# Expert stage of a hybrid block: the gather of token rows without transposes, two units at a time, in a written order

## The chip, the cores and the metric

The kernel runs on one core of one Trainium2 chip. The metric is the device time of one execution in microseconds (us). Engines are named as the profile names them: PE (TensorE matmul), PEld (its weight loads), DVE (VectorE), ACT (ScalarE), POOL (GpSimd), SP (the queue that issues the weight transfers).

## The reference

One block of a model with 256 tokens of 2048 features (float32): an adaptive norm, a wide projection, three mixers (stick-breaking attention, a diagonal state space layer, a chunked mLSTM), gated projections and an output projection, and then a mixture of 32 experts (4 groups of 8, two experts chosen per token inside the best group) and a last norm. The change is in the mixture:

```python
g_idx = jnp.argmax(g_logits, axis=-1)                       # best group of a token
top_v, top_i = lax.top_k(e_in_group, TOP_K)                 # two of its 8 experts
...
hid = jax.nn.silu(jnp.einsum('td,edf->tef', t, w1)) * jnp.einsum('td,edf->tef', t, w3)
y = jnp.einsum('tef,efd->td', hid * gates.astype(hid.dtype)[:, :, None], w2)
```

`t` is the normed and modulated row of a token; `w1`, `w3` are 32 x 2048 x 256, `w2` is 32 x 256 x 2048.

## The kernel before

Up to `x1`, the sum of the input and the gated mixers, the work is dense and is not touched. While `w_out` is multiplied, `split_x1` splits each 512 columns of `x1` into a high and a low part (`xs[0]`, `xs[1]`, type fp32r) so that later two fast products give the accuracy of float32: part 0 is an ACT copy, part 1 a DVE subtraction.

**Routing (the prologue).** After the last product of `w_out`, a written order for PE, DVE and ACT computes logits, the best group, the two experts and, per token and *list*, a rank. A list holds the tokens that choose one of two experts of a group (16 lists, up to 64 tokens each; more than 64 is handled in a branch that these inputs don't take). A *unit* `u` (8 of them) is two lists, so 128 rows. `mem` says whether a token is in a list, `rank` its place there.

**Gather.** `sel_unit(u)` builds a 0/1 matrix of 256 tokens x 128 places, four DVE operations of 64 columns. `Gather.rows(j)` multiplies it with `xs`: four products of 512 columns give 128 gathered rows of feature block `j` (512 features, four blocks). `scale(j)` (ACT) takes them out of PSUM and multiplies by the norm of each row, `norms()`; `turn(j)` transposes the four 128x128 pieces on PE (line 259, tile `xgT`); `finish(j)` applies the modulation of the features and writes four blocks of `XG`, two on ACT and two on DVE. The products of the experts need features on the partitions, hence the transposes. `gates()` fetches the weights of the rows, `back()` the transposed `sel` that brings results back to the tokens.

**Experts.** A unit is two *pairs* (`n` = 0 to 15, `u, el = divmod(n, 2)`); a pair is two experts, one for each list, and uses the two halves of the PE array, 64 columns each (`Pair.mm` issues each product twice, for h = 0 and h = 1 with `tile_position=(0, 64 * h)`). Per pair `mm_in(j)` for four blocks gives `h` (line 1397, float32, 512 columns), `hidden()` the activation, `hidden_turn()` two transposes and an ACT copy `hh`, and `mm_out(f, c)` for two halves of the hidden features and four column blocks gives `y` (line 1397 too). `combine_mm` brings the results of the unit before back to token order (`sc`), `combine_add` adds them to `x1`.

**Weights.** A pair reads 12 buffers of 1 MiB (`load_in`: 8, in two transfers each; `load_out`: 4). The ring (`moe_raw`) has 11 of them, all issued by SP in program order; a transfer starts when the product that last read its buffer has ended. So the first 11 are loaded ahead of the stage, and the rest follow the releases. The row `final_g` for the last norm is loaded by POOL into one of the ring's buffers (tag `raw`) when the last pair's `mm_in(3)` has released it.

**Order.** From the first pair on, the loop over `n` is written as in the diff, but a scheduler decides the order of each engine's instructions in it; the prologue and the last pair have a written order (`tc.manual_schedule`). PSUM has four buffers for `y` (`mm`) and four for all else (`ms`).

## Time and profile before

| | us |
|---|---|
| three runs | 1597.33, 1601.37, 1603.7 (median 1601.37) |
| the profiled execution | 1600.31 |
| its span, from the first to the last instruction | 1598.5 |
| the prologue (rank known to first expert product) | 1082.20 to 1093.02 |
| the pairs, first to last expert product | 1093.02 to 1579.79 |

The times of the profile count from the start of the span. Busy times of PE are of records that overlap, so the distance between starts says more than the length of one. Releasers of a wait are inferred from semaphores.

### The profile page before, as it was taken

What the parts mean: (1) busy time and instruction counts of PE and PEld (TensorE: products, weight loads), DVE (VectorE), ACT (ScalarE), POOL (GpSimd) and SP (SyncE); (2) the same over time, 40 slices, a digit from 0 to 9 for tenths busy, and PEclk for the clock granted to TensorE, in tenths of its full rate; (3) what the DMA queues carried; (4) which work ended last, traced back from release to release, by engine and by line L of the source; (5) the groups of instructions that cost most, each with busy time, mean ns of one, the idle gap of its engine ahead of it and who ended that gap; (6) DMA issues with size and microseconds to landing.
All of it is one profiled execution on the core that took longest, in us unless ns stands there. A gap on an engine that the chain in (4) does not pass through costs nothing.

```text
span 1598.5 us, 25021 instructions
## 1 busy us (share of the span) xinstructions
PE 1509.0 (94%) x10228; PEld 1140.2 (71%) x10228; DVE 1015.1 (64%) x1733; ACT 568.6 (36%) x755; POOL 39.0 (2%) x63
## 2 busy tenths in 40 slices
PE   4999999989999998999999999999999999999996
PEld 2999999888888988899999998874334433443332
DVE  0879997889879999999778866553213212222124
...
GB/s 343 386 348 305 319 191 222 220 223 261 247 300 265 229 264 231 273 264 264 263 308 327 318 267 241 207 228 257 414 413 412 413 402 374 412 392 411 404 412 183
DMA packets 172249, 488.13 MB, mean 305 GB/s; under 512 B 13876, under 2 KB 14048, under 8 KB 162784
## 3 DMA queue, kind: packets, MB, share of 16 engines
...
q0 software_dynamic: 3088, 12.14, 2.3%
...
q10 hardware_dynamic: 576, 1.05, 0.2%
...
## 4 chain that ended last, share of the span: by engine, by line
PE 54%; DVE 25%; DMA 10%; issue 6%; ACT 4%; POOL 0%; SPq 0%; ACTq 0%; DVEq 0%; POOLq 0%
PE h L1397 14%; PE y L1397 9%; DVE accr L353 5%; DMA adar<-in_w_ada_dram 4%; DVE g_sb_w L132 2%; DVE g_ml_w L132 2%; PE sc L1446 2%; PE wo_b L143 2%; PE wo_b L144 2%; PE wo_b L142 2%; DVE bu L698 2%; PE xg L1312 2%; DVE s5pp L695 2%; DVE bu L697 1%; DVE s5qq L696 1%
## 5 line engine op out<-in xcount | busy, mean ns | idle before, releaser
L1397 PE MATMUL h<-w,XG 128*64 128x512 f32 x1024 | 245.3, 599 | 0.0
L1397 PEld LDWEIGHTS h<-w,XG 128*64 128x64 f32 x1024 | 75.7, 137 | 139.1 <-issue 137.4
L353 DVE SCALAR_TENSOR_TENSOR accr<-adar,ccol,accr 128x1024 f32<-128x1024 f32 x120 | 153.5, 1280 | 18.2 <-DMA adar<-in_w_ada_dram 17.3
L1397 PE MATMUL y<-w,hh 128*64 128x512 f32 x512 | 150.4, 598 | 0.5 <-ACT hh L1419 0.5
L1410 DVE SCALAR_TENSOR_TENSOR s<-h,gg,s 128x256 f32<-128x256 f32 x16 | 7.7, 484 | 167.8 <-ACT s L1409 167.8
L1455 DVE TENSOR_TENSOR x<-x,sc 128x512 f32<-128x512 f32 x64 | 43.0, 682 | 105.7 <-PE sc L1446 105.7
L1397 PEld LDWEIGHTS y<-w,hh 128*64 128x64 f32 x512 | 49.0, 136 | 81.5 <-issue 77.7
L1409 ACT ACTIVATE s<-h 128x256 f32<-128x256 f32 x16 | 6.1, 383 | 212.3 <-PE h L1397 212.3
L144 PE MATMUL g_sb_b<-hT,g_sb_w 128*128 128x256 f32 x256 | 73.1, 285 | 8.5 <-DVE g_sb_w L132 8.4
L144 PE MATMUL g_ml_b<-hT,g_ml_w 128*128 128x256 f32 x256 | 72.4, 283 | 3.3 <-DVE g_ml_w L132 3.3
L1287 DVE TENSOR_SCALAR XG<-xgT,G,modc 128x128 f32<-128x128 f32 x64 | 26.0, 410 | 77.0 <-ACT XG L1284 77.0
L144 PE MATMUL g_s_b<-hT,g_s_w 128*128 128x256 f32 x256 | 72.1, 282 | 1.6 <-DVE g_s_w L132 1.4
L142 PE MATMUL g_ml_b<-hT,g_ml_w 128*128 128x256 f32 x256 | 72.4, 283 | 0.0
L142 PE MATMUL g_sb_b<-hT,g_sb_w 128*128 128x256 f32 x256 | 71.9, 281 | 0.0
L142 PE MATMUL g_s_b<-hT,g_s_w 128*128 128x256 f32 x256 | 71.7, 280 | 0.0
L143 PE MATMUL g_s_b<-hT,g_s_w 128*128 128x256 f32 x256 | 71.6, 280 | 0.0
L143 PE MATMUL g_ml_b<-hT,g_ml_w 128*128 128x256 f32 x256 | 71.5, 279 | 0.0
L143 PE MATMUL g_sb_b<-hT,g_sb_w 128*128 128x256 f32 x256 | 71.4, 279 | 0.0
L132 DVE TENSOR_TENSOR wo_w<-wo_w,wo_w 128x1024 fp32r<-128x1024 f32 x32 | 39.0, 1223 | 31.8 <-ACT wo_w L131 31.6
L303 DVE SCALAR_TENSOR_TENSOR acc<-ada,ccol,acc 128x1024 f32<-128x1024 f32 x45 | 57.6, 1281 | 0.5
L131 ACT CAST g_ml_w<-g_ml_w 128x1024 fp32r<-128x1024 f32 x32 | 32.0, 1048 | 70.4 <-DMA g_ml_w<-in_w_in_dram 47.4
L144 PEld LDWEIGHTS g_sb_b<-hT,g_sb_w 128*128 128x128 f32 x256 | 48.1, 188 | 11.2 <-DVE g_sb_w L132 11.1
...
## 6 DMA issues: line engine op xcount, KB each, us to landing
w<-in_moe_w_dram SPq DMA_DIRECT2D x256, 512.0 KB, 9.2
adar<-in_w_ada_dram SPq DMA_DIRECT2D x64, 1024.0 KB, 5.5
w<-in_moe_w_dram SPq DMA_DIRECT2D x64, 1024.0 KB, 9.9
...
g_sb_w<-in_w_in_dram SPq DMA_DIRECT2D x16, 1024.0 KB, 5.4
g_ml_w<-in_w_in_dram SPq DMA_DIRECT2D x16, 1024.0 KB, 5.4
g_s_w<-in_w_in_dram SPq DMA_DIRECT2D x16, 1024.0 KB, 6.1
wo_w<-in_w_out_dram SPq DMA_DIRECT2D x16, 1024.0 KB, 5.1
```

What stands on the lines that cost most here:

```text
L131: nc.scalar.copy(out=hv, in_=src)
L132: nc.vector.tensor_tensor(out=lv, in0=src, in1=hv.bitcast(F32), op=ALU.subtract)
L142: nc.tensor.matmul(o, lhsT=lhs[0], rhs=rhs[0], start=start, stop=False, **kw)
L143: nc.tensor.matmul(o, lhsT=lhs[0], rhs=rhs[1], start=False, stop=False, **kw)
L144: nc.tensor.matmul(o, lhsT=lhs[1], rhs=rhs[0], start=False, stop=stop, **kw)
L303: nc.vector.scalar_tensor_tensor(acc, raw[:, :, q], cs, acc, op0=ALU.mult, op1=ALU.add)
L353: nc.vector.scalar_tensor_tensor(acc, raw[:, q], cs, acc, op0=ALU.mult, op1=ALU.add)
L695: V.tensor_tensor(out=pp, in0=L2R, in1=prev, op=ALU.mult)
L698: V.tensor_tensor(out=cur, in0=cur, in1=qq, op=ALU.add)
L1312: nc.tensor.matmul(self.pt[j], lhsT=self.sel[:, tt], rhs=xs[i][:, tt, 512 * j:512 * j + 512], start=(i == 0 and tt == 0), stop=(i == 1 and ...
L1397: nc.tensor.matmul(o[sl, :], lhsT=lhsT[:, sl], rhs=rhs(h), start=start, stop=stop, tile_position=(0, 64 * h), skip_group_check=True)
L1455: V.tensor_tensor(out=x1[:, tt, sl], in0=x1[:, tt, sl], in1=pts[tt], op=ALU.add)
```

## The change

`Batch(b)` gathers two units (`2b`, `2b + 1`) at once, with the gathered rows as columns: `xs` becomes the stationary operand and `sel` (256 places) the moving one, so the result has features on the partitions and no transpose is needed. For that `split_x1` writes `xs` in block order (feature `4p + k` of a 512 block goes to place `128k + p`) and reads `x1` with a stride of 4. `sel` is one comparison per 128 tokens: `rank` is moved by -1000 for members of a list, and `iotam` counts from -1000. The norms come as a row of 256 on all partitions, by two float32 products, and DVE multiplies them in; ACT writes the blocks of the first unit, DVE those of the second. A batch is gathered every second unit (`u` = 1, 3, 5, during both its pairs), so three `X` buffers are needed: `XG2` shares its space with small tiles of the routing (`early`, `part`). Batch 0 has only `rows(0)` ahead of pair 0; `rows(1)` to `rows(3)` stand between the products of pair 0. The body of the loop is a written order for PE. The overflow branch follows the new layout.

```diff
+        hi, lo = (x[:, tt, sl].rearrange("p (k q) -> p k q", k=4) for x in xs)
         if part == 0:
-            nc.scalar.copy(out=xs[0][:, tt, sl], in_=x1[:, tt, sl])
+            nc.scalar.copy(out=hi, in_=src)
         else:
-            V.tensor_tensor(out=xs[1][:, tt, sl], in0=x1[:, tt, sl], in1=xs[0][:, tt, sl].bitcast(F32),
-                            op=ALU.subtract)
+            V.tensor_tensor(out=lo, in0=src, in1=hi.bitcast(F32), op=ALU.subtract)
...
     NU = 8
+    AWAY = 1000.0
+    iotam = pd.tile([P, 64], F32, name="iotam")
+    V.tensor_scalar(iotam, iota[:, 0:64], -AWAY, None, op0=ALU.add)
...
-    class Gather:
-
-
-        def __init__(self, u):
-            self.u = u
-            self.sel = sel_unit(u)
-            self.X = XG[:, u % 2]
-            self.x, self.pt, self.pT = {}, {}, {}
+    class Batch:
+
+
+        def __init__(self, b):
+            self.b = b
+            self.sel = pd.tile([P, 2, 256], F32R, tag="sel", bufs=2, name=f"sel{b}")
+            for tt in range(2):
+                V.tensor_tensor(out=self.sel[:, tt].rearrange("p (i s) -> p i s", i=4),
+                                in0=iotam[:, None, :].to_broadcast([P, 4, 64]),
+                                in1=rank[:, tt, 4 * b:4 * b + 4][:, :, None].to_broadcast([P, 4, 64]),
+                                op=ALU.is_equal)
+            self.units = [Unit(2 * b + i, self.sel[:, :, 128 * i:128 * i + 128]) for i in range(2)]
+            self.pt = {}
 
         def norms(self):
 
-            pt = psum("ms", f"r2p{self.u}")
+            pt = psum("ms", f"r2p{self.b}")
             for tt in range(2):
-                nc.tensor.matmul(pt[:, :1], lhsT=self.sel[:, tt].bitcast(F32), rhs=r2[:, tt:tt + 1], start=(tt == 0),
-                                 stop=(tt == 1))
-            self.r = pd.tile([P, 1], F32, tag="r2s", bufs=2, name=f"r2s{self.u}")
-            V.tensor_copy(out=self.r, in_=pt[:, :1])
+                nc.tensor.matmul(pt[:, :256], lhsT=r2[:, tt:tt + 1].to_broadcast([P, 128]),
+                                 rhs=self.sel[:, tt].bitcast(F32), start=(tt == 0), stop=(tt == 1))
+            self.r = pd.tile([P, 256], F32, tag="r2s", name=f"r2s{self.b}")
+            V.tensor_copy(out=self.r, in_=pt[:, :256])
 
         def rows(self, j):
-            self.pt[j] = psum("ms", f"xg{self.u}{j}")
-            for i in range(2):
-                for tt in range(2):
-                    nc.tensor.matmul(self.pt[j], lhsT=self.sel[:, tt], rhs=xs[i][:, tt, 512 * j:512 * j + 512],
-                                     start=(i == 0 and tt == 0), stop=(i == 1 and tt == 1))
-
-        def scale(self, j):
-            self.x[j] = pd.tile([P, 512], F32, tag="xgr", bufs=2, name=f"xgr{self.u}{j}")
-            nc.scalar.activation(self.x[j], self.pt.pop(j), AF.Copy, scale=self.r)
-
-        def turn(self, j):
-            self.pT[j] = psum("ms", f"xgT{self.u}{j}").rearrange("p (k s) -> p k s", k=4)
-            x = self.x.pop(j)
-            for kk in range(4):
-                transpose(self.pT[j][:, kk, :], x[:, kk::4], P)
+
+            for half in range(2):
+                pt = psum("ms", f"xg{self.b}{j}{half}").rearrange("p (q s) -> p q s", q=2)
+                for q in range(2):
+                    kk = 2 * half + q
+                    for n in range(4):
+                        i, tt = divmod(n, 2)
+                        nc.tensor.matmul(pt[:, q, :], lhsT=xs[i][:, tt, 512 * j + 128 * kk:512 * j + 128 * kk + 128],
+                                         rhs=self.sel[:, tt], start=(n == 0), stop=(n == 3), skip_group_check=True)
+                self.pt[j, half] = pt
 
         def finish(self, j):
-            modulate(self.pT.pop(j), j, self.X[:, 4 * j:4 * j + 4, :])
+            for half in range(2):
+                t = pd.tile([P, 512], F32, tag="xgr", bufs=2, name=f"xgr{self.b}{j}{half}") \
+                    .rearrange("p (q s) -> p q s", q=2)
+                V.tensor_tensor(out=t, in0=self.pt.pop((j, half)), in1=self.r[:, None, :].to_broadcast([P, 2, 256]),
+                                op=ALU.mult)
+                for q in range(2):
+                    k = 4 * j + 2 * half + q
+                    nc.scalar.activation(self.units[0].X[:, k, :], t[:, q, :128], AF.Identity,
+                                         bias=modc[:, 3, k:k + 1], scale=G2[:, k:k + 1])
+                    V.tensor_scalar(self.units[1].X[:, k, :], t[:, q, 128:], G2[:, k:k + 1], modc[:, 3, k:k + 1],
+                                    op0=ALU.mult, op1=ALU.add)
+
+    class Unit:
+        def __init__(self, u, sel):
+            self.u, self.sel = u, sel
+
+        @property
+        def X(self):
+            return XG[:, self.u % 3] if self.u % 3 < 2 else XG2
 
...
         V.tensor_tensor(out=dd, in0=v2, in1=v1, op=ALU.subtract)
         nc.scalar.activation(dd, dd, AF.Exp)
-        split_x1(0, 3, 1)
-        V.tensor_copy(out=rank, in_=prk[:, :32].rearrange("p (t s) -> p t s", t=2))
+        V.scalar_tensor_tensor(rank, mem.bitcast(F32), -AWAY, prk[:, :32].rearrange("p (t s) -> p t s", t=2),
+                               op0=ALU.mult, op1=ALU.add)
         XG = cp.tile([P, 2, 16, P], F32, tag="H0", name="XG")
-        ga = Gather(0)
-        ga.norms()
-        split_x1(1, 3, 1)
-        ga.rows(0)
-        ga.rows(1)
-        ga.scale(0)
-        ga.turn(0)
-        ga.rows(2)
-        ga.scale(1)
-        ga.finish(0)
-        ga.turn(1)
-        ga.rows(3)
-        ga.scale(2)
-        ga.finish(1)
+        ba = Batch(0)
+        ba.norms()
+        ba.rows(0)
+        ba.finish(0)
+        for tt in range(2):
+            split_x1(tt, 3, 1)
+
         gw = sm([P, 2], "gw")
         V.tensor_reduce(out=gw, in_=gx, axis=AX.X, op=ALU.add)
         V.reciprocal(gw, gw)
@@ -1563,13 +1578,8 @@
         V.tensor_tensor(out=oh2, in0=oh2, in1=dd[:, :, None].to_broadcast([P, 2, 8]), op=ALU.mult)
         within = sm([P, 2, 8], "within")
         V.tensor_tensor(out=within, in0=oh1, in1=oh2, op=ALU.add)
-        ga.turn(2)
-        ga.scale(3)
-        ga.finish(2)
-        ga.turn(3)
-        ga.finish(3)
-    ga.gates()
-    ga.back()
+    XG2 = pd.tile([P, 16, P], F32, tag="XG2", name="XG2")
+    ga = ba.units[0]
...
-    done = nxt = None
+    done = None
     for n in range(2 * NU - 1):
         cur = Pair(n, ga)
         u, el = cur.u, cur.el
-        gat = u + 1 < NU
+        gat = u % 2 == 1 and u + 1 < NU
         for j in range(4):
             cur.load_in(j)
         for f in range(2):
             cur.load_out(f)
-        cur.mm_in(0)
-        cur.mm_in(1)
-        if gat:
+        with tc.manual_schedule(engines={ENG.PE}):
+            cur.mm_in(0)
+            if n == 0:
+                ba.rows(1)
+                ba.finish(1)
+            cur.mm_in(1)
+            if n == 0:
+                ba.rows(2)
+                ba.finish(2)
+            if gat:
+                if el == 0:
+                    ba = Batch(u // 2 + 1)
+                    ba.norms()
+                ba.rows(2 * el)
+                ba.finish(2 * el)
+            cur.mm_in(2)
+            if gat:
+                ba.rows(2 * el + 1)
+                ba.finish(2 * el + 1)
+            if n == 0:
+                ba.rows(3)
+                ba.finish(3)
+                ga.gates()
+                ga.back()
+            cur.mm_in(3)
+            cur.hidden()
+            if done is not None:
+                combine_add(2 * el, combine_mm(done[0], done[1][el][:, 0], u - 1, 2 * el))
+            cur.hidden_turn()
             if el == 0:
-                nxt = Gather(u + 1)
-                nxt.norms()
-                nxt.gates()
-            nxt.rows(2 * el)
-            nxt.scale(2 * el)
-        cur.mm_in(2)
-        if gat:
-            nxt.rows(2 * el + 1)
-            nxt.scale(2 * el + 1)
-        cur.mm_in(3)
-        cur.hidden()
-        if done is not None:
-            combine_add(2 * el, combine_mm(done[0], done[1][el][:, 0], u - 1, 2 * el))
-        elif gat:
-            nxt.turn(2 * el)
-        cur.hidden_turn()
-        if done is not None and gat:
-            nxt.turn(2 * el)
-        if gat:
-            nxt.finish(2 * el)
-        if el == 0:
-            py = [psum("mm", f"y{u}_{c}") for c in range(4)]
-        for c in range(4):
-            cur.mm_out(0, c, py)
-        if gat:
-            nxt.turn(2 * el + 1)
-            nxt.finish(2 * el + 1)
-        if done is not None:
-            combine_add(2 * el + 1, combine_mm(done[0], done[1][el][:, 1], u - 1, 2 * el + 1))
-        for c in range(4):
-            cur.mm_out(1, c, py)
-        if el == 1:
-            yp = row_pairs(u)
+                py = [psum("mm", f"y{u}_{c}") for c in range(4)]
             for c in range(4):
...
```

Three places in the order of instructions. The first is PE in pair 2 (unit 1), the first half of its `y` products. `w_6_3` is the buffer of the expert in h = 0, `w_6_0` that of h = 1; `hh` are the hidden rows. Before:

```order
L1397 MATMUL y_0_11528<-w_6_3_11430,hh_11517 64x512
L1397 MATMUL y_1_11529<-w_6_3_11430,hh_11517 64x512
L1397 MATMUL y_2_11530<-w_6_3_11430,hh_11517 64x512
L1397 MATMUL y_0_11528<-w_6_0_11434,hh_11517 64x512
L1397 MATMUL y_1_11529<-w_6_0_11434,hh_11517 64x512
L1397 MATMUL y_2_11530<-w_6_0_11434,hh_11517 64x512
L1397 MATMUL y_3_11531<-w_6_3_11430,hh_11517 64x512
L1397 MATMUL y_3_11531<-w_6_0_11434,hh_11517 64x512
```

Behind the change, with the rows ahead of them (`sc` is `combine_mm`, `hT` the transposes of the hidden rows):

```order
L1468 MATMUL sc_11529<-yp_0_11362,selTs_11233 128x512 x2
L1468 MATMUL sc_11532<-yp_0_11362,selTs_11233 128x512 x2
L259 MATMUL hT_11537<-cst,s_2_11526 128x128 x2
L1419 MATMUL y_0_11542<-w_6_3_11413,hh_11540 64x512
L1419 MATMUL y_0_11542<-w_6_0_11417,hh_11540 64x512
L1419 MATMUL y_1_11543<-w_6_3_11413,hh_11540 64x512
L1419 MATMUL y_1_11543<-w_6_0_11417,hh_11540 64x512
L1419 MATMUL y_2_11544<-w_6_3_11413,hh_11540 64x512
L1419 MATMUL y_2_11544<-w_6_0_11417,hh_11540 64x512
L1419 MATMUL y_3_11545<-w_6_3_11413,hh_11540 64x512
L1419 MATMUL y_3_11545<-w_6_0_11417,hh_11540 64x512
```

Three products of one half of the array stood behind each other (in pairs 0, 1 and 15 the halves alternate before too); now they alternate, and `sc` stands ahead of `hT`.

The second is PE at the end of the prologue, from the last gather products to the first of pair 0 (`h` from `w_0_0`, h = 0, and `w_2_0`, h = 1). Before:

```order
L1312 MATMUL xg_11064<-xs_10250,sel_11020 128x512 x2
L259 MATMUL xgT_11087<-cst,xgr_11069 128x128 x4
L259 MATMUL xgT_11098<-cst,xgr_11092 128x128 x4
L1333 MATMUL gg_11108<-within,sel_11020 128x8 x2
L259 MATMUL selT_11114<-cst,sel_11020 128x128 x2
L1576 MATMUL cnt<-mem,cst 1x16 x2
L1397 MATMUL h_11157<-w_0_0_11126,XG 64x512
L1397 MATMUL h_11157<-w_2_0_11129,XG 64x512
```

Behind the change, from the norms products (`r2p`) on:

```order
L1312 MATMUL r2p_11018<-sel_11015,r_10246 128x256 x2
L1325 MATMUL xg_11023<-sel_11015,xs_10247 128x256 x2
L1325 MATMUL xg_11023<-sel_11015,xs_10248 128x256 x2
L1325 MATMUL xg_11023<-sel_11015,xs_10247 128x256 x2
L1325 MATMUL xg_11023<-sel_11015,xs_10248 128x256 x2
L1325 MATMUL xg_11032<-sel_11015,xs_10247 128x256 x2
L1325 MATMUL xg_11032<-sel_11015,xs_10248 128x256 x2
L1325 MATMUL xg_11032<-sel_11015,xs_10247 128x256 x2
L1325 MATMUL xg_11032<-sel_11015,xs_10248 128x256 x2
L1586 MATMUL cnt<-mem,cst 1x16 x2
L1419 MATMUL h_11109<-w_0_0_11076,XG 64x512
L1419 MATMUL h_11109<-w_2_0_11079,XG 64x512
```

Of the four feature blocks one is left ahead of the first `h`; the two transposes, `gg` and `selT` have moved behind it or are gone.

The third is DVE at the same time. Before, from the last split ahead of the rank to the first blocks of `XG`:

```order
L1237 TENSOR_TENSOR xs_10250<-x_10222,xs_10249 128x512
L1538 COPY rank_t<-rank 128x32
L1276 TENSOR_SCALAR sel_11020<-cst,rank_t,mem 128x64 x4
L1276 TENSOR_SCALAR sel_11174<-cst,rank_t,mem 128x64
L1306 COPY r2s_11028<-r2p_11025 128x1
L1237 TENSOR_TENSOR xs_10250<-x_10222,xs_10249 128x512
L1276 TENSOR_SCALAR sel_11174<-cst,rank_t,mem 128x64 x3
L1287 TENSOR_SCALAR XG<-xgT_11043,G_10238,modc 128x128 x2
```

Behind the change, from the end of `finish(0)` to the first operation of `finish(1)` (`xgr_11136`):

```order
L1248 TENSOR_TENSOR xs_10248<-x_10222,xs_10247 128x512 x2
L1570 TENSOR_REDUCE gw<-gx 128x2
L1591 CAST cnti<-cnt_11072 1x1
L1571 RECIPROCAL gw<-gw 128x2
L1573 TENSOR_SCALAR w1t<-dd 128x2
L1574 RECIPROCAL w1t<-w1t 128x2
L1575 TENSOR_TENSOR w1t<-w1t,gw 128x2
L1576 TENSOR_TENSOR dd<-dd,w1t 128x2
L1577 TENSOR_TENSOR e1oh<-e1oh,w1t 128x16
L1578 TENSOR_TENSOR e_oh<-e_oh,dd 128x16
L1580 TENSOR_TENSOR within<-e1oh,e_oh 128x16
L1333 TENSOR_TENSOR xgr_11136<-xg_11118,r2s_11021 128x512
```

Both splits of the last 512 columns and the chain from `gw` to `within` now stand between `finish(0)` and `finish(1)`.

## Rows read from the trace of the kernel before

**Rows 1.** The page of the profile, its first part: busy time of each engine, share of the span, instructions.

```profile
PE 1509.0 (94%) x10228; PEld 1140.2 (71%) x10228; DVE 1015.1 (64%) x1733; ACT 568.6 (36%) x755; POOL 39.0 (2%) x63
```

**Rows 2.** Busy time by stretch, one row for each: the stretch in us, its length, busy us and number of instructions of PE, PEld, DVE, ACT and POOL, the granted TensorE clock (1.00 is full speed), the mean busy share of the 16 DMA engines, and GB/s. The first is the prologue, the next two are the expert stage, the last is where the weights end.

```profile
1085.00:1099.00 14.00, 12.14 (x58) 7.48 (x58) 5.96 (x27) 5.99 (x13) 0.00 (x0) 0.88 0.01 5
1105.00:1280.00 175.00, 169.68 (x724) 67.90 (x722) 42.05 (x92) 33.27 (x65) 0.00 (x0) 1.00 1.02 413
1280.00:1565.00 285.00, 274.93 (x1148) 108.47 (x1145) 62.17 (x125) 41.56 (x84) 0.00 (x0) 1.00 1.00 401
1565.00:1575.00 10.00, 9.48 (x44) 3.64 (x44) 3.65 (x6) 2.86 (x5) 0.53 (x1) 1.00 0.67 249
```

**Rows 3.** Waits of SP, the queue that issues the weight loads, from 1099 to 1570: the engine and line that waits, the engine and line it waits for, us in total, times, the longest.

```profile
SPq L1377 <- PE h L1397: 83.4, 48, 5.1
...
SPq L1391 <- PE h L1397: 72.8, 14, 8.3
SPq L1391 <- PE y L1397: 51.7, 23, 4.1
```

**Rows 4.** Waits of TensorE's weight loads in the same stretch, with the same columns: the row of the `h` products that waits for a transfer of weights.

```profile
PEld h L1397 <- DMA w<-in_moe_w_dram: 1.5, 5, 0.4
```

**Rows 5.** The chain that ended last, pairs 2 to 4 (unit 1 and the first pair of unit 2): start us, length us, engine, tile, line, records merged. A plain float32 product is two records.

```profile
1164.59 2.58 PE h L1397 x10
...
1168.15 0.44 PE hT L259 x2
1168.59 0.48 PE xgT L259 x4
1169.07 4.55 PE y L1397 x16
1173.62 0.68 PE xgT L259 x4
1174.29 0.93 PE sc L1446 x4
1175.22 4.06 PE y L1397 x13
...
1180.57 2.07 PE xg L1312 x8
...
1187.34 10.48 PE h L1397 x48
...
1219.88 10.50 PE h L1397 x48
```

**Rows 6.** The same chain in pair 0.

```profile
1114.13 7.07 PE y L1397 x32
```

**Rows 7.** The timeline of PE in a projection ahead of the expert stage: start us, length us, line, tiles, shape of the weights and of the result. Products with 256 moving columns, each with its own weight load.

```profile
559.74 0.28 PE L142 MATMUL g_sb_b<-hT,g_sb_w 128*128 128x256 f32 x1
559.86 0.28 PE L143 MATMUL g_sb_b<-hT,g_sb_w 128*128 128x256 f32 x1
```

**Rows 8.** The timeline of all engines in the prologue, same columns; in square brackets the idle time of the engine before it and what ended that.

```profile
1082.02 1.11 PE L1499 MATMUL warm<-cst 128*128 128x512 f32 x2
1082.20 0.19 DVE L1538 COPY rank_t<-rank 128x32 f32<-128x32 f32 x1 [0.59 <-PE rank L1528]
1082.42 1.20 DVE L1276 TENSOR_SCALAR sel<-cst,rank_t,mem 128x64 fp32r<-128x64 f32 x5
...
1086.50 0.46 ACT L1284 ACTIVATE XG<-xgT,modc,G 128x128 f32<-128x128 f32 x1
...
1090.12 0.15 DVE L1555 TENSOR_REDUCE gw<-gx 128x2 f32<-128x8 f32 x1
...
1091.37 0.17 DVE L1565 TENSOR_TENSOR within<-e1oh,e_oh 128x16 f32<-128x16 f32 x1
...
1093.02 7.56 PE L1397 MATMUL h<-w,XG 128*64 128x512 f32 x26
...
1098.40 0.33 SPq L1391 DMA_DIRECT2D w<-in_moe_w_dram  x1
```

**Rows 9.** Busy time by stretch, with the columns of rows 2: two stretches at the end of the prologue, one in the stage before it, and the start of the weight stream.

```profile
1089.00:1093.00 4.00, 2.16 (x17) 1.45 (x15) 2.87 (x16) 2.45 (x6) 0.00 (x0) 1.00 0.00 0
1093.00:1096.60 3.60, 3.58 (x10) 1.67 (x12) 1.81 (x8) 0.46 (x1) 0.00 (x0) 0.53 0.02 5
968.00:972.00 4.00, 1.95 (x12) 1.42 (x11) 3.87 (x5) 1.05 (x1) 0.00 (x0) 1.00 0.00 0
1098.40:1101.00 2.60, 2.60 (x15) 1.28 (x13) 0.00 (x0) 0.00 (x0) 0.00 (x0) 1.00 0.63 164
```

**Rows 10.** Groups of instructions (the first over the whole span, the others from 1000 to 1600): line, engine, operation, tiles, shapes, count, busy us, mean ns of one, idle time before them and what ended it.

```profile
L259 PE MATMUL xgT<-cst,xgr 128*128 128x128 f32 x128 | 22.2, 296 | 1.1 <-ACT xgr L1317 1.1
...
L1410 DVE SCALAR_TENSOR_TENSOR s<-h,gg,s 128x256 f32<-128x256 f32 x16 | 7.7, 484 | 167.8 <-ACT s L1409 167.8
...
L1237 DVE TENSOR_TENSOR xs<-x,xs 128x512 fp32r<-128x512 f32 x7 | 4.8, 683 | 0.0
```

**Rows 11.** The chain in the last pair.

```profile
1571.36 5.37 PE y L1397 x24
```

**Rows 12.** The timeline at the same place, the load of `final_g`.

```profile
1569.99 0.53 POOL L1702 DMA_DIRECT2D fg<-in_final_g_dram  x1 [496.74 <-DMA w<-in_moe_w_dram]
```

**Rows 13.** DMA issues from 1000 to 1600: tile, source, issuing queue, count, KB each, median us from issue to landing.

```profile
fg<-in_final_g_dram POOLq DMA_DIRECT2D x1, 1024.0 KB, 5.1
```

57 lines of the change are left out of this document (33 added, 24 removed).

## The prediction

> **What bounds the kernel now.** I read the page first and then only the expert stage, since every edit lies there or just ahead of it. The page says little by itself: TensorE is busy for nearly the whole span [rows 1], which is an average over stages with different limits.
>
> The table by stretches divides the expert stage [rows 2]. In the prologue (1085 to 1099) the DMA engines move 5 GB/s: every weight buffer is full and waits to be read. From 1105 to 1280 they move 413 GB/s at a busy share of 1.02, and from 1280 to 1565 it is 401. So the weight stream runs almost at what it can do, and the kernel sits close to two bounds at once.
>
> The waits say which one ends last. SP stands in front of a buffer that a product has not yet released for 83.4 + 72.8 + 51.7 us [rows 3]; the weight loads of the `h` products wait for a transfer for 1.5 us in all [rows 4]. So TensorE is the bound, and the stream idles now and then because the ring is full. How near the second bound is: one pair takes 12 buffers of 1.0486 MB, which is 30.5 us at 413 GB/s (2.539 us a buffer). A pair now takes TensorE about 31.6 us: its last `h` product ends at 1167.17 in pair 2, at 1197.82 in pair 3 and at 1230.38 in pair 4, 30.65 and 32.56 us apart [rows 5].
>
> Then the chain of one pair [rows 5]. Its `h` products go at 10.48/48 = 0.218 us a record. Its `y` products do not: 16 records take 4.55 us and the next 13 take 4.06 us (0.28 and 0.31 us each). In pair 0 the same 32 records take 7.07 us, 0.221 each [rows 6]. The order of the program shows why they may differ: in pair 0 the two column halves of the array (experts h = 0 and h = 1) alternate, in the pairs from 2 to 14 three or four products of one half stand in a row.
>
> **Prologue, step by step.** Before, the rank is copied at 1082.20 and the first `h` product starts at 1093.02; SP issues into the first released buffer at 1098.40 [rows 8]. Between 1093 and 1096.6 the granted clock is 0.53, nearly all of it at 1.2 GHz, after a stretch (1089 to 1093) with TensorE busy for 2.16 of 4 us [rows 9].
>
> After, up to the first product: `rank` still ends at about 1082.4. Two `sel` operations of 128x256 have no row; five of 128x64 took 1.20 us (0.24 each), a 128x256 operation from PSUM 484 ns [rows 8, 10]; I take 0.4 each, to 1083.2. The two norms products are plain float32 over 256 columns; one such product over 512 columns (two records of `warm`) took 1.11 us, so half each, 1.1 together: 1084.3. The gather products have 256 moving columns and a new weight load each. The like of them in the projections starts every 0.117 us [rows 7], so the eight of the first half end at about 1085.4. The multiplication by the norm (512 wide, 683 ns [rows 10]), one ACT block (0.46 us [rows 8]) and hand-overs: the first `h` product at 1086.7, 6.3 us earlier. DVE writes two blocks of the other unit (0.8 us) before it takes the second half, whose blocks follow at 1088.0 and 1088.5, when the third and fourth block are needed, so `mm_in(0)` (16 records, 3.5 us) ends at 1090.2. The first release moves by 1098.4 - 1090.2 = 8.2 us. Bounds: 5.4 if the clock halves again in that stretch and a step is 1 us dearer; 9 if `sel` costs 0.24.
>
> What is given back: the other three blocks of pair 0 and pair 1 are now gathered between its products, and each `mm_in` waits on `rows`, one multiplication and one ACT block. DVE has more in front of `finish(1)`: two splits of 683 ns, and the chain from `gw` to `within` which took from 1090.12 to 1091.54 [rows 8, 10]. After `mm_in(0)` DVE is free 1.5 us later, then 0.7 and 0.5 us and hand-overs to the first block, and 3.5 us of products: 6.3 us. The next step, without the splits, is 6.1, the one with `gates` and `back` 6.7. These are the times from one release of two buffers to the next, and the stream takes 5.1 us for two: it idles there for about 4.2 us (bounds: 2 and 8).
>
> **Steady pairs.** Three parts, all on TensorE. The transposes go: 128 records, 22.2 us busy [rows 10]; in the pair shown 0.48 + 0.68 us. The gather itself costs the same: eight records of 512 columns took 2.07 us [rows 5] for one unit's half, sixteen of 256 columns cost 1.9 us for two units. The fixed order makes the `y` products alternate: 7.07 us for 9.5, 2.5 us a pair in 13 pairs. Between the last `h` and the transposes of the hidden rows TensorE waited 0.98 us (1167.17 to 1168.15); `combine_mm` (0.93 us) now stands in that gap. In turn nothing covers 1168.15 to 1169.07 but the transposes of 0.44 us.
>
> A pair with gather becomes: h 14.0, y 7.1, combine 1.9, gather 3.7, norms 0.5, hidden turn 0.9, the uncovered rest and `gates` 0.4: 28.5 us. A pair without gather: 24.3 us. Both are under the 30.5 us of the stream. So the bound changes: TensorE will wait for weights, 2 to 6 us a pair, and its gain beyond that is worth nothing. Where this cover is gone (a stream faster than 28.5 us a pair) the TensorE prices count again.
>
> The other edits I cost at nothing: the strided splits are ACT and DVE work (683 ns on DVE [rows 10]) beside a full TensorE, and if the stride doubled them, one on the path would add 0.7 us; the shared tile `early` is dead before `XG2` is written; DVE's 13 us of `finish` per batch (8 x 0.683 and 16 blocks at no more than ACT's 0.46) lie beside two pairs of products.
>
> **The sum.** It is made on the stream, since that ends last. 192 buffers less the 11 that are full are 181; at 2.539 us they take 459.5 us. Before: first issue 1098.4; 164 GB/s from there to 1101 is what a full stream moves in 1.0 us [rows 9], so it counts as full from 1100.0, 1.6 after the issue, and could have ended at 1559.5. It ended at 1568.5 (249 GB/s in 1565 to 1575 is 2.49 MB, of which 1.05 is the row `final_g` [rows 2, 13]): 9.0 us lost to full rings. The products that read the last two buffers, the third column block of the last `y`, begin at 1571.36 + 2/3 of 5.37 = 1574.9 [rows 11], 6.4 us later still. From there to the end at 1598.5 it is 23.6 us, and nothing in that is changed.
>
> After: full from 1090.2 + 1.6 = 1091.8, plus 459.5, plus 4.2 idle: 1555.5. One more cost: the load of `final_g` takes a `raw` buffer which is free when the last `mm_in(3)` ends. Before, that was after the weights had landed (issue at 1569.99, 5.1 us [rows 12, 13]). Now the last four weight buffers are still on their way, and 1.05 MB beside them delays them by 2.5 us: 1558.0. With an allowance of 1.0 for the last landing, and then 23.6, the span is 1582.6. The profiled execution took 1600.31 us for a span of 1598.5, so 1.8 us lie around it: 1584.4, which is 15.9 us under the profiled execution. That execution is 1.06 us under the median of the three runs, 1601.37; beside the median it would be 1585.5. I forecast 1585.
>
> The price that hangs most on one number is the rate: each 1% is 4.6 us. 401 GB/s, as from 1280 on, includes the pauses of the full ring, so it is a lower end.
>
> **Rivals.**
> *The stream does not reach 413.* If 401 GB/s is not the ring's doing but the memory's, 181 buffers take 473.3 us: 1585 + 13.8 = 1599, no change that shows. For it: 401 is what is measured over 285 us. Against: the waits of SP on products.
>
> *The prologue gives less.* With both lower ends (release 2.8 us later, idle 8 instead of 4.2 us): 1585 + 6.6 = 1592.
>
> *The clock falls (slower).* TensorE will stand still for some 1.5 us in each 5.1 us of two buffers. Before, 2.16 busy us of 4 were followed by 0.53; but 1.95 of 4 in 968 to 972 kept 1.00 [rows 9]. If the clock halved in a share s of the time, a pair would need 28.5 or 24.3 us, in the mean of six pairs with gather and ten without 25.9, divided by (1 - s/2). Above s = 0.36 that passes today's 31.6 us; at s = 0.5 it is 34.5 us, and 16 pairs cost 46 us more than before, less the 8 of the prologue: about 1640. Against it: a half clock makes TensorE the late one, it stops waiting, and the clock returns as at 1096.6. The Trainium skill ("TensorE: Matmul & The Clock Gate", "Loop structure matters more than you think") warns of this shape of loop, a DMA wait between products, as one that leaves the engine cold. By that rule this change would be the slow case; the trace has both outcomes, so it keeps a small chance.
>
> *The stream can go faster.* Nothing has pushed it for longer than the ring allowed. At 28.5 us for a pair with gather TensorE could take 441 GB/s. If the stream followed to that, it would take 430.4 us: 1585 - 29.1 = 1556. Against: the busy share is 1.02 at 413. The Trainium skill ("DMA: Bandwidth & Descriptors", "Specifications") gives 435 GB/s as the ceiling of the fabric, by which the end would be at an estimated 1562; the trace's long stretch lies 5% under it.
>
> **How the numbers follow.** Chances: forecast 0.70 (its own range 1578 to 1591), less in the prologue 0.12, 401 GB/s 0.09, clock 0.05, faster stream 0.04. A measurement of this kernel tells 0.5%, 8 us, from no change. Under 1593 lie the first, most of the second and the last: 0.84. Within 8 us of 1601 lie the third, the rest of the second and a mild clock loss: 0.12. Slower 0.04. The range of 1575 to 1596 leaves out the faster stream, the clock and most of 401 GB/s.
>
> **What would show it.** First `h` product near 1086.7 and SP's next issue near 1090; records of `y` at 0.22 us in all pairs; weight loads of `h` and `y` that wait for DMA for tens of us in all, where it was 1.5; SP waiting on products for far less than 208 us; 410 GB/s or more from 1110 to 1550, with the last issue some 14 us earlier. Wrong it would be if TensorE still never waits for a weight, if the clock column of the expert stage leaves 1.00, or if the stream's rate stays near 400 with SP not waiting on products.

## The result, and the profile after

The changed kernel takes 1590.8 us (median of four runs, 1588.5 to 1593.3), 0.9934 of the kernel before on the same chip (95% interval 0.9908 to 0.9959). A second comparison gave 0.9952 (0.9934 to 0.9970). So it is 8 to 11 us faster; 16.4 were forecast. The execution read below took 1592.7 us for a span of 1590.9.

The page, in the lines that answer to [rows 1]: the busy time of PE, the granted clock in 40 slices (in tenths, 9 is 90% or more) and the GB/s in the same slices of about 40 us.

```profile
PE 1474.4 (93%) x10212; PEld 1131.5 (71%) x10212; DVE 1030.6 (65%) x1738; ACT 551.7 (35%) x723; POOL 39.9 (3%) x63
...
PEclk9999999999999999999999999999999999999998
...
GB/s 341 386 347 303 331 182 230 218 220 271 222 288 275 237 241 267 230 276 261 266 309 336 325 282 216 235 180 281 396 415 412 413 414 413 412 413 414 412 412 191
```

PE is busy 35 us less, and from the 30th slice to the last but one the stream stands at 412 to 415 GB/s. The stretches of the expert stage, with the columns of [rows 2]:

```profile
1095.00:1125.00 30.00, 28.11 (x150) 16.18 (x151) 8.73 (x26) 7.58 (x16) 0.00 (x0) 1.00 0.91 323
1125.00:1280.00 155.00, 144.36 (x674) 60.13 (x671) 43.63 (x87) 20.80 (x45) 0.00 (x0) 1.00 1.02 413
1280.00:1540.00 260.00, 233.36 (x1045) 90.59 (x1045) 66.72 (x128) 30.08 (x66) 0.00 (x0) 1.00 1.02 413
1540.00:1560.00 20.00, 16.93 (x72) 6.54 (x68) 2.46 (x5) 0.48 (x2) 0.53 (x1) 1.00 1.03 409
1560.00:1565.00 5.00, 4.50 (x18) 1.33 (x18) 2.17 (x4) 2.63 (x5) 0.00 (x0) 1.00 0.84 334
1565.00:1570.00 5.00, 2.69 (x10) 1.14 (x10) 1.04 (x3) 0.37 (x1) 0.00 (x0) 1.00 0.06 25
```

Where it was 401 GB/s from 1280 on [rows 2], it is 413 to 1540. Only the start (323 GB/s from 1095 to 1125) and the very end are below. The granted clock is 1.00 in every stretch.

SP's waits from 1099 to 1570 (who waits for whom, us in total, times, longest), which answer to [rows 3]:

```profile
SPq L1399 <- DMA w<-in_moe_w_dram: 265.0, 219, 2.1
SPq L1413 <- DMA w<-in_moe_w_dram: 48.2, 52, 1.8
SPq L1399 <- PE h L1419: 15.7, 7, 5.0
SPq L1399 <- PE y L1419: 6.9, 12, 4.1
```

SP stood in front of unreleased buffers for 208 us. Now its waits on products are some 30 us, and those on transfers are over 310 (96 before). PE is the mirror image. These are its groups of `h` and `y` products from 1099 on: records, busy us and mean ns of one, then the idle time ahead of them and what ended it:

```profile
L1419 PE MATMUL h<-w,XG 128*64 128x512 f32 x1002 | 239.5, 597 | 32.4 <-DMA w<-in_moe_w_dram 31.9 <-ACT XG L1337 0.4
L1419 PE MATMUL y<-w,hh 128*64 128x512 f32 x512 | 117.9, 598 | 10.2 <-ACT hh L1441 7.8 <-DMA w<-in_moe_w_dram 2.5
```

The matmuls of `h` wait 31.9 us for weights (27 waits, the longest 1.9), and the weight loads of [rows 4], which waited 1.5 us, now wait 27.0. The `y` products were 150.4 us busy before and are now 117.9. The chain that ended last, which was products [rows 5], is weight transfers from 1182 to 1567. Its last transfer and the products behind it:

```profile
1549.63 17.64 DMA w<-in_moe_w_dram
...
1567.31 1.93 PE y L1419 x6
```

And the prologue, which answers to [rows 8]:

```profile
1086.80 0.19 DVE L1559 SCALAR_TENSOR_TENSOR rank_t<-mem,rank 128x32 f32<-128x32 f32 x1 [1.92 <-PE rank L1550]
1087.02 1.43 DVE L1301 TENSOR_TENSOR sel<-iotam,rank_t 128x256 fp32r<-128x256 f32 x4
...
1088.34 2.26 PE L1325 MATMUL xg<-sel,xs 128*128 128x256 f32 x16
...
1089.68 0.69 DVE L1333 TENSOR_TENSOR xgr<-xg,r2s 128x512 f32<-128x512 f32 x1 [0.53 <-PE xg L1325]
...
1090.95 3.72 PE L1419 MATMUL h<-w,XG 128*64 128x512 f32 x16 [0.17 <-ACT XG L1337]
...
1094.61 2.17 PE L1325 MATMUL xg<-sel,xs 128*128 128x256 f32 x16
1094.63 0.33 SPq L1413 DMA_DIRECT2D w<-in_moe_w_dram  x1
...
1097.20 3.72 PE L1419 MATMUL h<-w,XG 128*64 128x512 f32 x16 [0.43 <-ACT XG L1337]
```

From the rank to the first `h` product it is 4.15 us (10.8 before), to SP's first issue 7.83 (16.2). Then the steps: one `mm_in` starts at 1090.95, the next at 1097.20.

### The profile page after: what moved, and what is told of

Read it like the earlier page. It is cut to its first block, busy times and chain, and to the rows that moved or that the text cites. A ratio compares the mean times of both kernels' runs of the same rounds, so it can differ in the third digit from the quotient of the medians.

```text
span 1590.9 us, 24948 instructions
## 1 busy us (share of the span) xinstructions
PE 1474.4 (93%) x10212; PEld 1131.5 (71%) x10212; DVE 1030.6 (65%) x1738; ACT 551.7 (35%) x723; POOL 39.9 (3%) x63
## 3 DMA queue, kind: packets, MB, share of 16 engines
q10 hardware_dynamic: 576, 1.05, 0.2%
## 4 chain that ended last, share of the span: by engine, by line
PE 38%; DMA 34%; DVE 21%; ACT 4%; issue 2%; SPq 0%; DVEq 0%; ACTq 0%
DMA w<-in_moe_w_dram 24%; DVE accr L353 4%; DMA adar<-in_w_ada_dram 3%; PE h L1419 3%; DVE g_sb_w L132 2%; DVE g_ml_w L132 2%; PE wo_b L143 2%; PE wo_b L144 2%; DMA mlo_w<-in_w_in_dram 2%; PE wo_b L142 2%; PE y L1419 2%; DVE bu L698 2%; DVE s5pp L695 1%; DVE bu L697 1%; PE g_s_b L144 1%
## 5 line engine op out<-in xcount | busy, mean ns | idle before, releaser
L1419 PE MATMUL h<-w,XG 128*64 128x512 f32 x1024 | 244.6, 597 | 33.0 <-DMA w<-in_moe_w_dram 31.9
L1419 PEld LDWEIGHTS h<-w,XG 128*64 128x64 f32 x1024 | 82.8, 136 | 175.1 <-issue 142.7
L1419 PE MATMUL y<-w,hh 128*64 128x512 f32 x512 | 117.9, 598 | 10.2 <-ACT hh L1441 7.8
L1419 PEld LDWEIGHTS y<-w,hh 128*64 128x64 f32 x512 | 35.9, 136 | 74.8 <-issue 59.8
L1337 ACT ACTIVATE XG<-xgr,modc,G 128x128 f32<-128x128 f32 x64 | 28.1, 486 | 128.6 <-DVE xgr L1333 128.6
L1333 DVE TENSOR_TENSOR xgr<-xg,r2s 128x512 f32<-128x512 f32 x32 | 22.0, 687 | 64.5 <-PE xg L1325 64.5
```

What stands on the lines that cost most here:

```text
L1333: V.tensor_tensor(out=t, in0=self.pt.pop((j, half)), in1=self.r[:, None, :].to_broadcast([P, 2, 256]), op=ALU.mult)
L1337: nc.scalar.activation(self.units[0].X[:, k, :], t[:, q, :128], AF.Identity, bias=modc[:, 3, k:k + 1], scale=G2[:, k:k + 1])
L1419: nc.tensor.matmul(o[sl, :], lhsT=lhsT[:, sl], rhs=rhs(h), start=start, stop=stop, tile_position=(0, 64 * h), skip_group_check=True)
```

## The experiments

The time at which `rank` is ready drifts by several us from one execution to the next (1077.9 to 1087.2 us over all profiles). The table therefore also gives *rank to end*: the span less that time, which removes what happens ahead of the gather. *Rank to pair 15* ends earlier, at the activation of the hidden rows of the last pair.

| kernel | ratio to before (95%) | median us | rank to pair 15, us | rank to end, us |
|---|---|---|---|---|
| before | | 1598.2 to 1602.5 | 487.2 | 516.3 |
| changed | 0.9934 and 0.9952 | 1590.8, 1590.7 | 471.6, 470.6 | 504.1, 503.1 |
| before, order written | 0.9947 (0.9930 to 0.9964) | 1590.9 | 473.7 | 507.8 |
| changed, order free | 0.9936 (0.9915 to 0.9956) | 1588.5 | 469.8 | 503.9 |
| changed, rows ahead | 0.9985 (0.9968 to 1.0001) | 1595.6 | 477.7 | 510.4 |

Two stretches at a lower granted clock lie inside some of these spans, each worth 1.6 to 1.7 us. In the profile of the kernel before, the clock was 0.53 from 1093 to 1096.6 [rows 9], and the first 32 records of `h` took 8.85 us; with the order written it was 1.00 there, and the same records, behind the same code, took 7.16 us. At the end TensorE waits 2.5 us for the last weights, in the changed kernel as in the two with one half of the change. The six `y` records behind that wait took 1.93 us in the changed kernel, at a clock of 1.00. With the order written they took 2.98 us:

```profile
1564.86 2.98 PE L1397 MATMUL y<-w,hh 128*64 128x512 f32 x6 [2.50 <-DMA w<-in_moe_w_dram]
```

A stretch across them (columns of [rows 2]) has the clock at 0.50:

```profile
1566.00:1568.00 2.00, 2.00 (x5) 0.39 (x3) 0.13 (x1) 0.00 (x0) 0.00 (x0) 0.50 0.00 0
```

With the order free it was 3.47 us (clock 0.52 from 1564 to 1566). At the start the code is the same, so that difference is not the order's doing; whether the edits have a part in the fall at the end is not shown.

### Each half of the change alone

The order alone, on the kernel before:

```diff
+        with tc.manual_schedule(engines={ENG.PE}):
-        cur.mm_in(0)
+            cur.mm_in(0)
 ... the same for the rest of the loop's body, nothing else
```

> The kernel before, with its own gather, transposes and prologue, and only the order of the products in the loop over pairs written out as the code states it, so that the y products of the two column halves alternate. Theory (TensorE was the bound by about 1 us a pair, and the y products take 2.5 us a pair too long): TensorE falls to about 29 us a pair, the stream of weights becomes the bound, the 9.0 us lost to full rings go but for the 2.5 us of final_g beside the last buffers: some 6 us faster than before, 1595. Rival 1 (it is the gather without transposes that relieves TensorE, order alone does nothing): same as before, 1601. Rival 2 (the written order uncovers waits, the hidden rows' turn and the transposes' copies, that the scheduler had filled with products of the next pair): 3 us a pair more, so about as slow as before or slower, 1601 to 1620.

The new gather alone, without the written order:

```diff
-        with tc.manual_schedule(engines={ENG.PE}):
-            cur.mm_in(0)
+        cur.mm_in(0)
 ... the same for the rest of the loop's body, nothing else
```

> The changed kernel with the written order of the loop taken out, so that the scheduler places the products of the pairs. The y products stand in rows of one half again, at 0.28 to 0.31 us. Theory (the relief of both parts is more than is needed): a pair with gather takes TensorE about 31 us, one without 27, 28.4 in the mean, under the stream's 30.5; with 11 buffers of ring the stream goes on, 1591 to 1594. Rival (the alternation of the y products is what makes the stream the bound): TensorE again 31 us or more a pair, SP waits on products for 100 us or more, 1598 to 1602.

The order alone gave 0.9947, some 8 us: the theory's 6 us and 2 more. From rank to end it is 8.5 us, in which the 1.7 us gained by the clock at the start and the 1.6 us lost by it at the end about cancel. Its products from 1099 on:

```profile
L1397 PE MATMUL h<-w,XG 128*64 128x512 f32 x998 | 241.7, 597 | 18.7 <-DMA w<-in_moe_w_dram 18.7
L1397 PE MATMUL y<-w,hh 128*64 128x512 f32 x512 | 119.0, 601 | 4.5 <-DMA w<-in_moe_w_dram 2.5 <-ACT hh L1419 2.0
```

`y` falls to 119.0 us with the old gather and its transposes still there, and `h` waits for DMA: the stream is already the bound. With the order left free and the new gather, `y` stays slow:

```profile
L1419 PE MATMUL y<-w,hh 128*64 128x512 f32 x512 | 142.5, 603 | 3.0 <-DMA w<-in_moe_w_dram 2.5 <-ACT hh L1441 0.5
```

Yet that kernel is as fast as the changed one. The starts of the hidden rows' activation in its pairs 3 to 7 show why (start us, length us; one per pair, so their distances are the pace):

```profile
1198.11 0.38 ACT L1431 ACTIVATE s<-h 128x256 f32<-128x256 f32 x1 [9.69 <-PE h L1419]
...
1225.50 0.38 ACT L1431 ACTIVATE s<-h 128x256 f32<-128x256 f32 x1 [12.48 <-PE h L1419]
...
1252.00 0.38 ACT L1431 ACTIVATE s<-h 128x256 f32<-128x256 f32 x1 [24.64 <-PE h L1419]
...
1285.71 0.38 ACT L1431 ACTIVATE s<-h 128x256 f32<-128x256 f32 x1 [9.80 <-PE h L1419]
...
1317.57 0.38 ACT L1431 ACTIVATE s<-h 128x256 f32<-128x256 f32 x1 [9.69 <-PE h L1419]
```

27.4, 26.5, 33.7 and 31.9 us: 29.9 in the mean (28.4 was expected), just under the stream's 30.5. So either half lifts TensorE out of the way, and the second one adds nothing to the pace. What the gather adds to the order is the earlier start of the stream. SP's first issue comes 7.83 us after the rank instead of 14.5 with the order alone, 6.7 us earlier, and 4.3 us more are lost behind it in the steps between the first releases (6.9 us in place of 2.6, worked out from 323 and 354 GB/s in 1095 to 1125). That leaves 2.4 us, and 2.6 are found from the rank to pair 15 (473.7 to about 471.1). The rest of the 507.8 to about 503.6 is the clock at the end. The times do not tell the changed kernel from the order alone: the intervals of 0.9947, 0.9934 and 0.9952 overlap.

### Is the stream the bound now, and what was it before?

The loads of half of `w2` left out, in both kernels:

```diff
             self.raw["o", f] = []
+            if f == 1 and self.n < 2 * NU - 1:
+                self.raw["o", 1] = self.raw["o", 0]
+                return
```

> The changed kernel without the loads of the second half of w2 in pairs 0 to 14 (the products of f = 1 read the buffers of f = 0 again, so that part of the result is left out): ten buffers a pair, 25.4 us of stream. Theory (the stream is the bound now): 45 to 76 us faster than the changed kernel, 1515 to 1546, where the upper end is TensorE as the next bound at 25.9 us a pair in the mean. Rival (TensorE is still the bound): no change.

> The kernel before without the same loads (the second half of w2 in pairs 0 to 14 left out, the products read the first half's buffers). Theory (before, TensorE was the bound at 31.6 us a pair): little change, 0 to 10 us faster, 1590 to 1600. Rival (before, the stream was already the bound and the change only moved its start): 45 us faster or more, as for the changed kernel.

The changed kernel came to 0.9631 (1539.2 us), 51 us faster: fewer bytes are time, until TensorE is the bound. Its paces in the steady pairs (4 to 8) are then TensorE's own (the weight loads of `h` wait for DMA 1.9 us in all):

```profile
1219.41 0.38 ACT L1434 ACTIVATE s<-h 128x256 f32<-128x256 f32 x1 [12.37 <-PE h L1422]
...
1243.49 0.38 ACT L1434 ACTIVATE s<-h 128x256 f32<-128x256 f32 x1 [22.22 <-PE h L1422]
...
1273.91 0.38 ACT L1434 ACTIVATE s<-h 128x256 f32<-128x256 f32 x1 [1.66 <-PE h L1422]
...
1302.50 0.38 ACT L1434 ACTIVATE s<-h 128x256 f32<-128x256 f32 x1 [1.66 <-PE h L1422]
...
1327.52 0.39 ACT L1434 ACTIVATE s<-h 128x256 f32<-128x256 f32 x1 [12.35 <-PE h L1422]
```

24.1 and 25.0 us without gather, 30.4 and 28.6 with it: 27.0 in the mean. The kernel before gained only 7 us, 0.9955 (0.9929 to 0.9982):

```profile
1136.73 0.39 ACT L1412 ACTIVATE s<-h 128x256 f32<-128x256 f32 x1 [2.87 <-PE h L1400]
...
1163.46 0.39 ACT L1412 ACTIVATE s<-h 128x256 f32<-128x256 f32 x1 [2.87 <-PE h L1400]
...
1190.53 0.39 ACT L1412 ACTIVATE s<-h 128x256 f32<-128x256 f32 x1 [2.87 <-PE h L1400]
...
1222.87 0.38 ACT L1412 ACTIVATE s<-h 128x256 f32<-128x256 f32 x1 [8.39 <-PE h L1400]
...
1253.77 0.38 ACT L1412 ACTIVATE s<-h 128x256 f32<-128x256 f32 x1 [12.16 <-PE h L1400]
```

From pair 4 on its pace is 32.3 and 30.9 us, as with all loads [rows 5]: TensorE was the bound, as predicted. Pairs 2 and 3 come at 26.7 and 27.1 us, though, where the full kernel needed 29.6 and 30.6, and that is nearly all of the 7 us. It isn't the bytes: in neither kernel does a product of these pairs wait for a transfer for more than 0.4 us. The order of this kernel is the scheduler's, and with other loads it came out otherwise. The chain in pair 2 here:

```profile
1165.34 3.64 PE y L1400 x16
...
1170.59 3.58 PE y L1400 x16
```

These are the `y` products that took 4.55 and 4.06 us (for three fewer) before [rows 5]; here the halves alternate in this pair. So it is the same cause once more, and the experiment on the kernel before is not as clean as it was meant to be.

More TensorE work, once and twice:

```diff
-            cur.mm_in(0)
+            for _ in range(2 if n else 1):      # the second kernel: 3 if n else 1
+                cur.mm_in(0)
```

> The changed kernel with the 16 records of mm_in(0) issued twice in pairs 1 to 14 (the second time starts the sum again, so nothing else changes): 3.6 us more of TensorE a pair, 50 us in all. Theory (the stream is the bound and TensorE has 2 us to spare in a pair with gather and 6 us in one without, so 28.5 + 3.6 and 24.3 + 3.6, 29.5 us in the mean of a loop under the stream's 30.5): no change, 1588 to 1593. Rival (TensorE is still the bound, or so near that the ring can't cover it): 20 to 50 us slower.

> The changed kernel with the 16 records of mm_in(0) issued three times in pairs 1 to 14: 7.2 us more of TensorE a pair. Theory: 35.7 us a pair with gather, 31.5 without, about 33.1 in the mean, which passes the stream's 30.5 by 2.6 us: TensorE is the bound again, some 35 to 42 us slower, 1625 to 1633, and the weight loads of h no longer wait for DMA. Rival (TensorE has more to spare than worked out): less than 20 us slower.

50 us more of TensorE changed nothing: 0.9952, rank to end 504.3. The steady pairs of that kernel come at 33.9, 32.0, 28.5 and 27.5 us, 30.5 in the mean, which is the stream's own pace. 100 us more made 1636.5 us, 1.0239, 46 us over the changed kernel and a little over the expectation, which had TensorE's own pace at 26 us; the weight loads of `h` wait for DMA 1.9 us in all, where it was 27.0. So TensorE has about 3.5 us a pair to spare (30.5 less 27.0), and what goes beyond is paid nearly in full: 14 pairs of 7.2 - 3.5 us are 52.

### How much the early start is worth

All four blocks of the first batch gathered ahead of pair 0, as before the change:

```diff
         ba.finish(0)
+        for j in (1, 2):
+            ba.rows(j)
+            ba.finish(j)
         for tt in range(2):
             split_x1(tt, 3, 1)
+        ba.rows(3)
+        ba.finish(3)
 ... and the three `if n == 0: ba.rows(j); ba.finish(j)` go from the loop
```

> The changed kernel with the interleaving undone: all four row blocks of the first batch are gathered ahead of the first pair. Theory (the stream ends at the latest of the release times less what it can catch up): the first release comes 6 us later, but the next three follow at 3.7 us instead of 6.3, so the stream ends only 2.5 us later: 1593 to 1594. Rival 1 (each us that the first release moves is a us of the end): 6 us, 1597. Rival 2 (the prologue counts for nothing, TensorE's relief alone made the gain): 1591.

It came out nearer to rival 1 in size: 0.9985, rank to end 6.8 us longer. The size of the move was misjudged; the theory's rule, with the measured moves put in, fits. The prologue of this kernel:

```profile
1083.93 6.34 PE L1325 MATMUL xg<-sel,xs 128*128 128x256 f32 x50
...
1092.70 2.04 DVE L1248 TENSOR_TENSOR xs<-x,xs 128x512 fp32r<-128x512 f32 x2
...
1098.06 5.34 PE L1419 MATMUL h<-w,XG 128*64 128x512 f32 x20
...
1102.58 0.33 SPq L1413 DMA_DIRECT2D w<-in_moe_w_dram  x1
```

The first product comes 15.7 us after the rank (1082.38), and SP issues 20.2 us after it, 12.4 us later than in the changed kernel instead of the 6.3 assumed: the four blocks go at DVE's 2.5 us a block, and the last waits for two splits. About 2 us of the 12.4 are the clock, which was 0.50 from 1093 to 1099, at and behind a wait of 3.55 us for the splits: 13 gather records took 3.14 us there, and the first 16 of `h` 4.5 us. From the first release the stream is soon full (412 GB/s from 1105 to 1125). The changed kernel loses 6.9 us at its start, 5.3 beside the 1.6 of starting up; 12.4 - 5.3 = 7.1 us is what the theory's rule then gives, rival 1's gives 12.4, and 6.8 was found. Without the fall of the clock the early start would be worth less than 5 us, an estimate from these numbers.

### The load of `final_g`

```diff
-    nc.gpsimd.dma_start(out=fg, in_=A["final_g"]...)
+    nc.sync.dma_start(out=fg, in_=A["final_g"]...)
```

> The changed kernel with the load of final_g issued by SP behind the last weight loads instead of by POOL. Theory (its 1.05 MB beside the last four weight buffers delay those by 2.5 us): the weights land at about 1564.7 instead of 1567.3 in the profile's time and the end comes 2.5 us earlier, 1588. Rival 1 (the last buffers are late for another reason, such as the wide rows of the last w2 loads): no change, 1591. Rival 2 (the load now lands too late for the last multiplication): slower, by what the first yo waits for it.

> The changed kernel as it is, on the chip of the next run, for a comparison of the two. Expected from the runs so far: 0.993 to 0.995 of the kernel before, and rank to the end 504 us in the profile whenever rank itself comes (it came between 1080.7 and 1086.8 us in runs with the same code ahead of it); if the 1086.8 of the first profile was the change's doing, rank comes near 1086 again.

> The changed kernel with the load of final_g behind the last weight loads on SP's queue, a second time, beside the changed kernel on the same chip. Theory (rank to the end was 500.5 us in its first profile and 504.1 in that of the changed kernel): 3.6 us faster than the changed kernel, a ratio to before lower by 0.002. Rival (the difference of the first profiles is chance): the same ratio.

The last transfer in the chain with the load behind the weights, against that of the changed kernel above:

```profile
1542.44 15.25 DMA w<-in_moe_w_dram
```

The last transfer takes 15.25 us from its issue, where it was 17.64: 2.4 us. The second profile of the changed kernel has 17.69; the second with the load behind has 15.23, and the variant of the next section with the load behind 15.25. Rival 2 does not show: the first `yo` starts 12.3 to 12.4 us after the last weights in both kernels. In time: 0.9929 (0.9908 to 0.9950), then 0.9919 (0.9901 to 0.9937) against 0.9952 (0.9934 to 0.9970) on one chip, with medians of 1585.1 and 1590.7; rank to end 500.5 and 501.0. The intervals still touch, but together with the trace a gain of 2 to 3 us stands. This is the fastest version measured: one queue name more than the change, 0.992 to 0.993 of the kernel before.

As to `rank`: the code ahead of it is the same in all variants of the changed kernel but those of the next section, and it came at 1081.59 in the second profile. Of the 5.2 us between them 3.7 lie ahead of the `w_out` stage (its first multiplication by the gate starts at 995.12 and 991.44), and 1.5 behind it, where the last logits ran at a granted clock of 0.50 in the first profile and 1.00 in the second. The same kernel gave both.

### The splits in block order

The splits contiguous as before, the stride in the gather's weight loads instead:

```diff
-        src = x1[:, tt, sl].rearrange("p (q k) -> p k q", k=4)
+        src = x1[:, tt, sl]
...
-    lhsT=xs[i][:, tt, 512 * j + 128 * kk:512 * j + 128 * kk + 128]
+    lhsT=xs[i][:, tt, 512 * j + kk:512 * j + 512:4]
```

> The changed kernel with the splits of x1 contiguous as before and the stride in the gather's weight loads instead. Theory (the strided splits, 1.09 and 1.12 us where they were 0.68 and 0.60, delay the weight splits behind them and so cost 0.9 us in the w_out stage: from the first to the last multiplication by the gate there it was 79.64 to 79.67 us in nine profiles of the changed order and 78.75 to 78.77 in three of the order before): 78.8 us again; rank to the first h product stays 4.15 us if a weight load of every fourth column costs what a contiguous one does, and the whole is 0.9 us faster, too little for the times to tell. Rival 1 (the 0.9 us have another cause, such as the tiles that now share a buffer): 79.65 us stays. Rival 2 (the strided weight loads are slower): the 64 records of a batch take more than 0.117 us each, rank to the first h product passes 5 us.

> The same, and the load of final_g behind the last weight loads on SP's queue. Theory: both gains add up, rank to the end 500.5 to 501.0 us as in the two profiles with that load behind, the stage ahead 0.9 us shorter; 4 us faster than the changed kernel, 0.991 to 0.993 of the kernel before. Rival: strided weight loads give the 3 us back, 0.995.

First the stage ahead: the first and the last multiplication by the gate in the changed kernel,

```profile
995.12 1.28 DVE L1213 TENSOR_TENSOR ot<-wo_b,gb 128x512 f32<-128x512 f32 x2
...
1074.76 0.69 DVE L1213 TENSOR_TENSOR ot<-wo_b,gb 128x512 f32<-128x512 f32 x1 [0.71 <-PE wo_b L144]
```

79.64 us apart, and with contiguous splits

```profile
990.47 1.28 DVE L1213 TENSOR_TENSOR ot<-wo_b,gb 128x512 f32<-128x512 f32 x2
...
1069.27 0.69 DVE L1213 TENSOR_TENSOR ot<-wo_b,gb 128x512 f32<-128x512 f32 x1 [0.70 <-PE wo_b L144]
```

78.80, as in the kernel before (78.75). So the strided splits do cost 0.9 us. But the gather's products (records, busy us, mean ns), in the changed kernel and then here:

```profile
L1325 PE MATMUL xg<-sel,xs 128*128 128x256 f32 x192 | 26.4, 290 | 0.0
```

```profile
L1325 PE MATMUL xg<-sel,xs 128*128 128x256 f32 x192 | 48.3, 403 | 0.0
```

Products whose weight load reads every fourth column take nearly twice as long: 16 records start to end in 3.99 us where it was 2.1 to 2.3. The first product comes 5.64 us after the rank, and the steps between the first releases are 7.5 us instead of 6.25. Rank to pair 15 is 476.6 us, 5.5 more than in the changed kernel, which is what these steps add up to (1.5 and three times 1.3). Rank to end is 510.9 us, 7.3 more; the other 1.6 us are the clock once more:

```profile
1565.29 3.49 PE L1419 MATMUL y<-w,hh 128*64 128x512 f32 x6 [2.52 <-DMA w<-in_moe_w_dram]
```

The time is 0.9969 of the kernel before, and 0.9942 with `final_g` behind (rank to end 506.5, 5.5 to 6 us more than the same load gave with block order, at a full clock). Rival 2 holds. The block order of the splits is needed: it costs 0.9 us where ACT and DVE prepare weights and saves some 5.5 in the prologue.

## Why the prediction was right, and where it was off

The time lies in the range and the direction is right, and so is the main step, that the bound moves from TensorE to the stream. Point by point:

- **The stream's rate.** 413 GB/s was taken, and 413 came (1125 to 1540). The 401 of [rows 2] was the full ring's doing; that rival is out.
- **`y` at 0.22 us.** 150.4 to 117.9 us, 2.5 us in 13 pairs, as put. The order alone brings it (119.0), and so does the scheduler's own order where the halves alternate (pair 2 without half of `w2`), so its cause is the alternation.
- **TensorE per pair.** 28.5 us with gather and 24.3 without were forecast; 29.5 and 24.6 were measured with the stream out of the way. What the sum did not say: one half would have been enough.
- **The prologue.** 4.5 us to the first product, and 4.15 came; 8.0 to the first release, and 7.83 came. Steps of 6.3, 6.1 and 6.7 us were put; 6.25, 6.25 and 6.37 came. Of the 8.4 us by which the first release moved, 1.7 hang on the clock of 0.53 in the profile from which the forecast was made. Three profiles have that prologue; two show the fall, and the one with the order written does not, so this part of the gain is luck.
- **`final_g`.** 2.5 us were put, 2.4 found.
- **The tail.** 23.6 us put, 23.6 found (1567.31 to 1590.9).

The forecast was 6 us too good. From rank to end 500.4 us were forecast (1582.6 - 1082.2), and 504.1 and 503.1 came; the rest lies ahead of the rank. These steps were mis-sized:

- The start of the stream. 1.6 + 4.2 = 5.8 us were allowed, 6.9 were lost (323 of 413 GB/s in 30 us is 6.5, and 0.4 ahead of 1095). 1.1 us.
- The last landing. 1.0 us was allowed. 334 GB/s in 1560 to 1565 is 1.0 us lost, and the 2.3 us from 1565 to 1567.3, at 55 GB/s and a DMA share of 0.13, another 2.0: 3.0 us. A share of 0.13 is about two of the 16 engines, which still move the last buffer when the others have ended. 2.0 us.
- The strided splits ahead of the rank, costed at nothing as "beside a full TensorE". They grew from 683 to 1086 ns (DVE) and from 604 to 1125 (ACT), and ACT and DVE also prepare the weights that TensorE multiplies there. 0.9 us, in each of nine profiles.
- That is 4.0 of 6 us. The rest lies within what `rank` drifts. In four of nine profiles with the strided splits the last logits took 1.7 to 1.9 us instead of 1.08 (granted clock 0.50 to 0.59), and the rank came 12.0 to 12.2 us after the last multiplication by the gate instead of 10.5; a fifth had logits of 1.49 us and the rank at 10.5. In the three profiles of the kernel before and its variants, and the two with contiguous splits, it was always 10.5. Whether the change has a part in that wasn't settled.

The rival of the falling clock is out for the stream, where it was put. TensorE waits 32 us on transfers ahead of matmuls of `h` alone, in stalls of up to 1.9 us, and the granted clock stays 1.00 (2.4 GHz) from 1095 to 1570. The rule of the Trainium skill quoted in the prediction ("TensorE: Matmul & The Clock Gate", "Loop structure matters more than you think") speaks of a long DMA wait between products, and "long" is the word that the prediction left out; at these stalls the trace shows no fall. At other places of these runs the clock did fall to about 0.5 behind a wait: behind the 2.5 us for the last weights in three variants, though not in the changed kernel with the same wait, and behind the 3.55 us with the rows ahead. The faster stream is out too: with 3.5 us a pair of TensorE to spare the rate stayed at 413.
